# First projections of a two-layer decoder trunk: packing, loading and splitting of the first weights in another order

## The chip, the core and the metric

One core of a Trainium2 chip runs the whole program in one launch. The metric is device time in microseconds (us), the median of three runs. PE is the matrix engine, with its weight load (PEld) shown apart; DVE, ACT and POOL are the vector, scalar and general engines; SP issues most of the loads. Every engine has a queue of its own that it works through in order, and loads can be issued from SP's queue or ACT's.

## The reference, cut to what matters

A decoder trunk of two layers on one sequence of 256 tokens with 1024 channels in float32. Layer 0 has two groups of attention heads behind one input projection; only its beginning matters here.

```python
h = h + even_mixer(rmsnorm(h, even_norm1), even_w_in, ...)      # layer 0
h = h + conv_ffn(rmsnorm(h, ffn_norm[0]), ...)
h = h + odd_mixer(rmsnorm(h, odd_norm1), odd_w_in, ...)         # layer 1
h = h + conv_ffn(rmsnorm(h, ffn_norm[1]), ...)
return rmsnorm(h, final_norm)

def even_mixer(h, w_in, ...):
    qa, ka, va, qd, kd, vd = split_cols(h @ w_in, (512, 512, 512, 512, 512, 512))
    o_a = softmax(qa @ ka.T * 64**-0.5 + relative_bias, causal) @ va     # 8 heads of 64
    o_b = softmax(1) @ vd - lam * softmax(2) @ vd                        # 4 differential heads
    return concat(o_a, o_b) @ w_out
# lam = exp(sum(lp0*lp1)) - exp(sum(lp2*lp3)) + lam_init, from the input diff_lambda
```

## The kernel before, in words

**Numbers.** A float32 product is made of three matmuls. A weight is split into a high part (ACT copies it to a rounded type, `whi`, line 152) and a low part (DVE subtracts, `wlo`, line 153); the activations likewise into `xh` (ACT, line 234) and `xl` (DVE, line 236), both in the tile `xs`. A product is high x xh + high x xl + low x xh, accumulated in one bank (`pd`). All products go through the helper on line 123, so their rows carry that line.

**Norm.** The activations are multiplied by the norm's gain only (`gcol`, a small load on ACT's queue). The factor 1/rms of each token is put on behind the product: squares (`sqt`), their sums over channels by a product with ones (`pss`, PE), scale and epsilon (`rs`, DVE), power -0.5 (`r_col`, POOL), a diagonal matrix (`diag`, DVE), its product with ones (`psb`, PE), and a copy (`r_bc`, DVE). `stats1` (line 555) issues the steps to `diag`, `stats2` (line 559) those behind. `r_q` is `r_bc` times the score scale. `evac_pair` (line 516, operation on 518) multiplies a bank of q or k by it and so makes two heads' `qk`.

**Weights.** All weights lie in memory as chunks of at most 1 MB in the order of a list, PLAN (line 61). A chunk is [128 partitions, k tiles x columns]; a k tile is 128 channels. Three raw buffers (`raw`) rotate, as do four pairs of high and low buffers. `need(name)` (line 170) is called by a step that uses a chunk: it issues raw loads up to three chunks ahead and splits up to two ahead. A raw load waits until the low part of the chunk that had its buffer is done.

**The start.** The first chunks are q0, k0, q1, k1, each 256 columns by all 8 k tiles; then two chunks of v, and so on. x and the chunks q0 and k0 come in four pieces of two k tiles each (`FIRST_KS`, 256 KB a load). Chunk 3 (k1) goes to four small tiles of its own (`raw_t`). Nine warm-up matmuls run on PE, then for each piece xh, xl, the splits of both chunks and 24 matmuls: 96 up to k tile 7. Then come the bias table's row product (`psbt`) and four units: `u1` and `u2` with 24 matmuls each on q1, `u3` and `u4` with 24 each on k1. `stats1` stands at the end of `u2`, `stats2` and three evacuations at the end of `u3`, the fourth at the end of `u4`. Behind them are the units of v and of the later q and k, and `interleave` (line 493) puts the attention of a pair of heads between units: scores (`pS`, PE), bias and maximum (`sc`, `nm`, DVE), exponential (`ex`, ACT), scaling by the sum (`ex`, DVE), transposes (`pT`, PE), their copy (`pt`, ACT), the product with v (`pO`, PE). Task t may not begin before unit `FIRST` = 4.

**Other loads.** `bias_load` (line 327) reads a bias table `Tt` for some heads from memory, on ACT's queue. `loads`, in front of unit 6, issues lam's input (`lam_t`, line 1007) among others, on SP; `lambdas` (line 580), in front of unit 10, works it out on DVE (lines 582, 585, 588, 589) and ACT (line 587).

**What sets the order.** PE's instructions stand as written, in the whole program. For ACT, DVE, POOL and SP the framework's scheduler chooses the order, except in the stretch between the opening of `begin` (a manual schedule, line 977) and `begin.close()` in `u3`, where it is as written. The first loads are written ahead of that opening. Each engine starts an instruction only when those ahead of it in its queue have been started.

## Time and profile before

| | us |
|---|---|
| three runs, median | 603.11 (602.80 to 603.61) |
| profiled execution | 603.49 |
| its span, first to last instruction | 601.7 |
| PE busy | 590.3 |
| DVE busy | 441.5 |
| ACT busy | 348.7 |
| chain that ended last: share of PE | 88% |

The profiled execution is 1.79 us longer than its span. A row of the timeline gives start, duration, engine, source line, operation, output and inputs with their shapes, the count where neighbours are grouped, and in brackets the idle time of the engine ahead of it with what ended that idle time. The chain of waits gives start, duration and what the end waited for. A count of x4 with a time is the time from the first one's start to the last one's end.

### The profile page before, as it was taken

The page shows a single profiled execution, that of the slowest core. Times are in us where ns is not written, and L with a number is a line of the kernel's source. Part 1 is how long each engine was busy: PE and PEld are TensorE (multiplying, and loading weights), DVE is VectorE, ACT ScalarE, POOL GpSimd, SP SyncE. Part 2 cuts the span into 40 slices and gives each one's busy share as a digit, 9 for nine tenths or more (in the row PEclk, how much of TensorE's full clock was granted, in tenths as well). Part 3 has the DMA queues.
Part 4 walks back from the last instruction along what each step waited for, and adds up shares of the span by engine and source line. Part 5 has one row for each costly group of instructions (what it writes and reads, how often), then busy time and mean ns, then how long its engine had stood idle before and what let it go on. Part 6 is the DMA issues. An engine that isn't in the chain of part 4 may idle for free.

```text
span 601.7 us, 10374 instructions
## 1 busy us (share of the span) xinstructions
PE 590.3 (98%) x4076; PEld 544.2 (90%) x4076; DVE 441.5 (73%) x791; ACT 348.7 (58%) x645; POOL 69.6 (12%) x81
## 2 busy tenths in 40 slices
PE   7999999999999999999999999999999999999996
PEld 7988999999999999999999998999988888888885
DVE  5589667689877787777787885658967787777752
ACT  6648557466655565655664674736655566655632
POOL 1000000032101110011033100005111111011110
PEclk9999999999999999999999999999999999999998
DMA  8865653335455545544445434334545544554301
GB/s 300 298 230 217 242 182 148 141 136 191 164 211 210 192 169 199 209 160 167 172 171 205 145 141 141 141 141 162 219 145 209 210 167 183 211 179 171 141 1 71
DMA packets 20265, 106.67 MB, mean 177 GB/s; under 512 B 2478, under 2 KB 5496, under 8 KB 8568
## 3 DMA queue, kind: packets, MB, share of 16 engines
q1 hardware_dynamic: 16424, 101.40, 46.6%
q10 hardware_dynamic: 3632, 4.08, 2.0%
q8 instruction: 32, 0.52, 0.3%
q0 software_dynamic: 160, 0.52, 0.3%
q14 instruction: 17, 0.14, 0.1%
HBM read 104.92 MB, written 1.08 MB: 176 GB/s over the span
## 4 chain that ended last, share of the span: by engine, by line
PE 88%; DVE 4%; issue 3%; POOL 2%; ACT 2%; DMA 1%; SPq 0%; POOLq 0%; ACTq 0%; DVEq 0%
PE pd L123 51%; PE acc L123 26%; PE pv L123 4%; PE pO L123 2%; PE pS L123 2%; DVE wlo L153 2%; DMA raw<-in_wpack_dram 1%; PE puq L123 1%; POOL sqt L245 1%; DVE ex L363 1%; PE pukv L123 0%; DVE sc L353 0%; PE pT L367 0%; PE psb L123 0%; PE pss L123 0%
## 5 line engine op out<-in xcount | busy, mean ns | idle before, releaser
L123 PE MATMUL pd<-xs,whi 128*128 128x256 f32 (+1 forms) x1312 | 330.7, 332 | 2.5 <-ACT whi L152 2.5
L123 PE MATMUL pd<-xs,wlo 128*128 128x256 f32 x928 | 257.1, 282 | 0.0
L153 DVE TENSOR_TENSOR wlo<-raw,whi 128x1024 fp32r<-128x1024 f32 (+1 forms) x193 | 233.8, 1238 | 23.6 <-ACT whi L152 23.5
L123 PEld LDWEIGHTS pd<-xs,whi 128*128 128x128 f32 x1312 | 221.4, 192 | 25.7 <-ACT whi L152 3.1
L152 ACT ACTIVATE whi<-raw 128x1024 fp32r<-128x1024 f32 (+1 forms) x193 | 193.7, 1031 | 60.8 <-PE pd L123 20.9
L123 PEld LDWEIGHTS pd<-xs,wlo 128*128 128x128 f32 x928 | 175.0, 191 | 0.0
L123 PE MATMUL acc<-o,whi 128*128 128x256 f32 x608 | 108.7, 281 | 0.0
L123 PEld LDWEIGHTS acc<-o,whi 128*128 128x128 f32 x608 | 92.7, 188 | 1.0 <-issue 0.2
L123 PE MATMUL acc<-o,wlo 128*128 128x256 f32 x304 | 84.7, 279 | 0.0
L905 ACT ACTIVATE lowp<-pd 128x256 f32<-128x256 f32 x68 | 25.9, 380 | 79.8 <-PE pd L123 79.8
L801 POOL TENSOR_TENSOR ge<-ge,gbuf 128x256 f32<-128x256 f32 x44 | 37.0, 842 | 291.3 <-ACT ge L800 291.3
L906 DVE TENSOR_TENSOR ug<-pd,lowp 128x256 f32<-128x256 f32 x68 | 28.6, 420 | 50.3 <-ACT lowp L905 50.3
L123 PE MATMUL acc<-whi,o 128*128 128x512 f32 (+1 forms) x220 | 58.2, 350 | 0.2 <-ACT o L806 0.2
L123 PEld LDWEIGHTS acc<-o,wlo 128*128 128x128 f32 x304 | 57.1, 188 | 0.0
L123 PEld LDWEIGHTS acc<-whi,o 128*128 128x128 f32 x220 | 38.3, 188 | 7.5 <-ACT o L806 0.7
L123 PE MATMUL acc<-wlo,o 128*128 128x512 f32 (+1 forms) x110 | 38.6, 351 | 0.0
L356 ACT ACTIVATE ex<-sc,nm 128x256 f32<-128x256 f32 (+1 forms) x56 | 24.7, 443 | 17.7 <-DVE nm L353 14.3
L807 DVE TENSOR_TENSOR o<-ge,o 128x256 fp32r<-128x256 f32 x44 | 19.0, 439 | 21.5 <-ACT o L806 21.5
L788 ACT ACTIVATE t<-gbuf,ccol 128x256 f32<-128x256 f32 x44 | 26.4, 601 | 12.1 <-DVE gbuf L929 10.2
L806 ACT ACTIVATE o<-ge 128x256 fp32r<-128x256 f32 x44 | 18.4, 418 | 23.1 <-POOL ge L801 23.0
L123 PE MATMUL pv<-whi,xs 128*128 128x512 f32 x96 | 30.2, 395 | 0.0
L800 ACT ACTIVATE ge<-t 128x256 f32<-128x256 f32 x44 | 17.9, 410 | 15.3 <-DVE t L795 15.3
(153 smaller groups left out, 507.2 us busy)
## 6 DMA issues: line engine op xcount, KB each, us to landing
raw<-in_wpack_dram SPq DMA_DIRECT2D x91, 1024.0 KB, 4.8
raw<-in_wpack_dram SPq DMA_DIRECT2D x6, 256.0 KB, 5.3
raw<-in_wpack_dram SPq DMA_DIRECT2D x3, 512.0 KB, 5.6
Tt<-btab ACTq DMA_DIRECT2D x3, 512.0 KB, 7.1
raw_t<-in_wpack_dram SPq DMA_DIRECT2D x4, 256.0 KB, 6.4
Tt<-btab ACTq DMA_DIRECT2D x1, 1024.0 KB, 10.6
hT<-in_x_dram SPq DMA_DIRECT2D x3, 256.0 KB, 5.3
raw<-in_wpack_dram ACTq DMA_DIRECT2D x2, 256.0 KB, 5.0
```

What stands on the lines that cost most here:

```text
L123: nc.tensor.matmul(o, l, r, start=start, stop=stop, skip_group_check=True)
L152: nc.scalar.activation(hi[:, s], raw, AF.Copy)
L153: nc.vector.tensor_tensor(lo[:, s], raw, hi[:, s].bitcast(F32), op=ALU.subtract)
L245: eng.tensor_tensor(sqs['a'], sqs['a'], t, op=ALU.add)
L356: nc.scalar.activation(e[:, a:b], t[:, a:b], AF.Exp, bias=nm[:, i:i + 1], scale=-1.0, accum_out=den[:, i:i + 1])
L788: nc.scalar.activation(t1, g[:, 2:], AF.Identity, bias=col(f, 3), scale=col(f, 2))
L800: nc.scalar.activation(ge, t3, AF.Gelu)
L801: nc.gpsimd.tensor_tensor(ge, ge, gbuf[f % 3][:, 0, 2:], op=ALU.mult)
L806: nc.scalar.activation(o[:, 0], ge, AF.Copy)
L807: nc.vector.tensor_tensor(o[:, 1], ge, o[:, 0].bitcast(F32), op=ALU.subtract)
L905: nc.scalar.activation(lowp, p[:, S:], AF.Copy)
L906: nc.vector.tensor_tensor(t[:, i], p[:, :S], lowp, op=ALU.add)
```

## The change

It reorders the beginning of layer 0 in five ways; the matmuls, splits and loaded bytes are the same.

1. The first four chunks become q (512 columns) of k tiles 0 to 3 (`eqa`), q of k tiles 4 to 7 (`eqb`), and k likewise (`eka`, `ekb`). `pieces` cuts chunk 0 into four of one k tile, the others into two.
2. `FIRST_KS` is now one k tile each for the first four and two pieces of two: x comes in six loads, and the first 96 matmuls (all q) go in six parts.
3. `begin` opens ahead of the first loads, so that these stand in the written order on SP and ACT.
4. Units `u1` to `u4` become three: `u1` has the 48 matmuls of k tiles 0 to 3 of k, then `stats1`; `u2` 12 matmuls, `stats2`, 12 matmuls, three evacuations; `u3` the last 24 and the fourth evacuation. `FIRST` is 3, and `loads` and `lambdas` stand in front of units 5 and 9.
5. `split_piece(4, ...)` for the first half of chunk 4 stands behind `stats1`; the other half and chunk 5 stand behind the three evacuations.

```diff
-FIRST = 4
+FIRST = 3
-FIRST_KS = ((0, 2), (2, 4), (4, 6), (6, 8))
+FIRST_KS = ((0, 1), (1, 2), (2, 3), (3, 4), (4, 6), (6, 8))
...
-    for n, c in (("q0", 0), ("k0", 512), ("q1", 256), ("k1", 768)):
-        add("e" + n, "we_in", 0, 0, 8, c, 256)
+    for n, c in (("q", 0), ("k", 512)):
+        for i in range(2):
+            add(f"e{n}{'ab'[i]}", "we_in", 0, i * 512, 4, c, 512)
...
-        if i < 2:
-            return n, [slice(a * S, b * S) for a, b in FIRST_KS]
-        step = 512 if i == SMALL_RAW else 1024
+        step = 512 if i in (0, SMALL_RAW) else 1024
...
-    nc.scalar.activation(scr, ones[:, 0:1], AF.Copy)
+    begin = ExitStack()
+    begin.enter_context(tc.manual_schedule(engines={mybir.EngineType.Activation, mybir.EngineType.DVE,
+                                                  mybir.EngineType.Pool, mybir.EngineType.SP}))
...
     load_x(0, nc.sync)
     load_raw(0, 0, nc.scalar)
-    load_raw(1, 0)
-    load_x(1, nc.scalar)
+    nc.scalar.activation(scr, ones[:, 0:1], AF.Copy)
+    load_x(1, nc.sync)
     load_raw(0, 1)
-    load_raw(1, 1, nc.scalar)
-    for part in range(2, len(FIRST_KS)):
-        load_x(part, nc.sync)
-        for i in range(2):
-            load_raw(i, part)
+    load_x(2, nc.scalar)
+    load_raw(0, 2)
+    load_x(3, nc.scalar)
+    load_raw(0, 3)
+    for i in range(2):
+        load_x(4 + i, nc.sync)
+        load_raw(1, i)
     load_raw(2, 0)
...
-    def passmajor(items, ks):
+    def passmajor(name, items, ks):
         for n in range(3):
-            for ap, first, (hi, lo), c in items:
+            for ap, first, c in items:
                 s = slice(c, c + 128)
                 for k in ks:
+                    hi, lo = chunks[name + 'ab'[k // 4]]
                     w, m = ((hi, xh), (hi, xl), (lo, xh))[n]
-                    mm(ap, w[:, k, s], m[:, k], k == 0 and n == 0 and first, k == KD - 1 and n == 2)
+                    mm(ap, w[:, k % 4, s], m[:, k], k == 0 and n == 0 and first, k == KD - 1 and n == 2)
...
         def u1():
-            c = chunks['eq1']
-            p = box['q1'] = bank("pd")
-            colmajor([(p[:, 0:S], True, c, 0)])
+            box['k'] = [bank("pd"), bank("pd")]
+            for ks in ((0, 1), (2, 3)):
+                passmajor("ek", tiles(box['k']), ks)
             split_chunk(3)
...
+            stats1(env)
+            open_split(4)
+            split_piece(4, pieces(4)[1][0])
 
         def u2():
-            p = box['q1']
-            colmajor([(p[:, S:], True, chunks['eq1'], 128)])
-            stats1(env)
-
-        def u3():
-            box['k1'] = bank("pd")
-            colmajor([(box['k1'][:, 0:S], True, chunks['ek1'], 0)])
-            p = box['q1']
+            t = tiles(box['k'])[:2]
+            passmajor("ek", t, (4, 5))
             stats2(env)
             stats_q(env)
+            passmajor("ek", t, (6, 7))
             evac_pair(env, first[0], ('q0', 'q1'), env['r_q'])
-            evac_pair(env, first[1], ('k0', 'k1'), env['r_bc'])
-            evac_pair(env, p, ('q2', 'q3'), env['r_q'])
-            split_chunk(4)
-            split_at[0] = 5
+            evac_pair(env, box['k'][0], ('k0', 'k1'), env['r_bc'])
+            evac_pair(env, first[1], ('q2', 'q3'), env['r_q'])
+            split_piece(4, pieces(4)[1][1])
+            split_chunk(5)
+            split_at[0] = 6
             begin.close()
...
-        before(6, loads)
-        before(10, lambda: lambdas(box['lam']))
+        before(5, loads)
+        before(9, lambda: lambdas(box['lam']))
...
     for part, (a, b) in enumerate(FIRST_KS):
         make_xhat(range(a, b), NORM1[0])
-        for i in range(2):
-            split_piece(i, pieces(i)[1][part])
-        passmajor(items, range(a, b))
+        split_piece(part // 4, pieces(part // 4)[1][part % 4])
+        passmajor("eq", tiles(first), range(a, b))
```

How this moves instructions is seen in each engine's order. On SP at the program's start, `hT` is x and `raw` the chunks; the number behind a name tells buffers apart. Before (`raw_98` is chunk 0, `raw_100` chunk 1, `raw_111` chunk 2):

```order
L200 DMA hT_96<-in_x_dram 128x512
L144 DMA raw_98<-in_wpack_dram 128x512
L200 DMA hT_96<-in_x_dram 128x512
L144 DMA raw_100<-in_wpack_dram 128x512
L144 DMA raw_98<-in_wpack_dram 128x512
L144 DMA raw_100<-in_wpack_dram 128x512
L200 DMA hT_96<-in_x_dram 128x512
L144 DMA raw_98<-in_wpack_dram 128x512
L144 DMA raw_100<-in_wpack_dram 128x512
L144 DMA raw_111<-in_wpack_dram 128x1024
```

And after, with one x load of k tile 0 and one of k tile 1 in the first row, and `raw_99`, `raw_109` and `raw_113` for chunks 0, 1 and 2:

```order
L201 DMA hT_97<-in_x_dram 128x256 x2
L143 DMA raw_99<-in_wpack_dram 128x512 x3
L201 DMA hT_97<-in_x_dram 128x512
L143 DMA raw_109<-in_wpack_dram 128x1024
L201 DMA hT_97<-in_x_dram 128x512
L143 DMA raw_109<-in_wpack_dram 128x1024
L143 DMA raw_113<-in_wpack_dram 128x1024
```

ACT's queue has the first piece of chunk 0 and x of k tiles 2 and 3 now; before, it had the first piece of chunk 0, the second of x and the second of chunk 1. On SP, pieces of two chunks alternated; now one chunk comes whole before the next.

On DVE from the norm's first step to the fourth evacuation, before (`wlo_425` is chunk 4's low part, `wlo_435` chunk 5's):

```order
L252 TENSOR_SCALAR rs_382<-pss_378 128x2
L268 TENSOR_TENSOR diag_385<-ident_85,r_col_381 128x256
L286 COPY r_bc_414<-psb_412 128x256
L564 TENSOR_SCALAR r_q_416<-r_bc_414 128x256
L518 TENSOR_TENSOR qk_418<-pd_156,r_q_416 128x512
L518 TENSOR_TENSOR qk_420<-pd_157,r_bc_414 128x512
L518 TENSOR_TENSOR qk_422<-pd_317,r_q_416 128x512
L153 TENSOR_TENSOR wlo_425<-raw_295,whi_424 128x1024 x2
L153 TENSOR_TENSOR wlo_435<-raw_297,whi_434 128x1024 x2
L518 TENSOR_TENSOR qk_464<-pd_387,r_bc_414 128x512
```

And after (`wlo_385` is chunk 4's, `wlo_427` chunk 5's):

```order
L255 TENSOR_SCALAR rs_379<-pss_375 128x2
L271 TENSOR_TENSOR diag_382<-ident_85,r_col_378 128x256
L152 TENSOR_TENSOR wlo_385<-raw_291,whi_384 128x1024
L289 COPY r_bc_402<-psb_400 128x256
L568 TENSOR_SCALAR r_q_404<-r_bc_402 128x256
L522 TENSOR_TENSOR qk_418<-pd_156,r_q_404 128x512
L522 TENSOR_TENSOR qk_420<-pd_313,r_bc_402 128x512
L522 TENSOR_TENSOR qk_422<-pd_157,r_q_404 128x512
L152 TENSOR_TENSOR wlo_385<-raw_291,whi_384 128x1024
L152 TENSOR_TENSOR wlo_427<-raw_293,whi_426 128x1024 x2
L522 TENSOR_TENSOR qk_460<-pd_314,r_bc_402 128x512
```

One low part of 1024 columns has moved to between `diag` and `r_bc`; three are left between the third and the fourth evacuation.

On SP around lam's load, before (`raw_526` is chunk 7, `raw_867` chunk 11):

```order
L144 DMA raw_526<-in_wpack_dram 128x2048
L144 DMA raw_534<-in_wpack_dram 128x2048
L144 DMA raw_686<-in_wpack_dram 128x2048
L144 DMA raw_785<-in_wpack_dram 128x2048
L1007 DMA lam_t_681<-in_lam_dram 128x256
L144 DMA raw_867<-in_wpack_dram 128x2048
```

And after (`raw_522` is chunk 7, `raw_863` chunk 11):

```order
L143 DMA raw_522<-in_wpack_dram 128x2048
L143 DMA raw_530<-in_wpack_dram 128x2048
L143 DMA raw_682<-in_wpack_dram 128x2048
L143 DMA raw_781<-in_wpack_dram 128x2048
L143 DMA raw_863<-in_wpack_dram 128x2048
L1008 DMA lam_t_677<-in_lam_dram 128x256
L143 DMA raw_984<-in_wpack_dram 128x2048
```

`lam_t`'s load now stands behind chunk 11's raw load, which waits for the last low part of chunk 8 (`wlo_685` after, `wlo_689` before).

## Rows read from the trace of the kernel before

**Rows 1.** The page's first part: busy time of each engine, its share of the span, and its instructions.

```profile
PE 590.3 (98%) x4076; PEld 544.2 (90%) x4076; DVE 441.5 (73%) x791; ACT 348.7 (58%) x645; POOL 69.6 (12%) x81
```

**Rows 2.** Waits of PE over the whole run, and of its weight load from 5 to 70 us: who waited for whom, us in total, times, longest us.

```profile
PE pd L123 <- ACT whi L152: 2.5, 2, 1.7
PE pT L367 <- DVE lam_t L582: 1.1, 1, 1.1
...
PEld pS L123 <- DVE nm L353: 0.4, 1, 0.4
```

**Rows 3.** Timeline of PE through the first 96 matmuls, and the bias product behind them.

```profile
6.98 1.22 PE L123 MATMUL pd<-xs,whi 128*128 128x256 f32 x4 [1.73 <-ACT whi L152]
9.01 2.93 PE L123 MATMUL pd<-xs,whi 128*128 128x256 f32 x12 [0.81 <-ACT whi L152]
11.73 1.91 PE L123 MATMUL pd<-xs,wlo 128*128 128x256 f32 x8
13.44 2.36 PE L123 MATMUL pd<-xs,whi 128*128 128x256 f32 x16
15.63 1.12 PE L123 MATMUL pd<-xs,wlo 128*128 128x256 f32 x8
...
22.44 0.49 PE L123 MATMUL psbt<-oh_t,rb 32*20 32x384 f32 x1
```

**Rows 4.** The stretch of the first 96 matmuls as one window: its length, busy time and count of PE, PEld, DVE, ACT and POOL, then granted clock, the DMA engines' share and GB/s.

```profile
6.98:22.44 15.46, 14.65 (x96) 14.22 (x96) 9.79 (x16) 12.45 (x23) 0.00 (x0) 1.00 1.00 373
```

**Rows 5.** Timeline of ACT at the start.

```profile
5.03 0.91 ACT L234 ACTIVATE xs<-hT,gcol 128x256 fp32r<-128x256 f32 x2 [2.35 <-DMA gcol<-in_small_dram]
6.29 0.63 ACT L152 ACTIVATE whi<-raw 128x512 fp32r<-128x512 f32 x1 [0.36 <-DMA raw<-in_wpack_dram]
8.33 0.63 ACT L152 ACTIVATE whi<-raw 128x512 fp32r<-128x512 f32 x1 [1.40 <-DMA raw<-in_wpack_dram]
```

**Rows 6.** Loads at the start: SP's second issue in its timeline; the same load in the list of issues (queue, count, KB, us from issue to landing); and one piece of the chain of waits (start, us, what).

```profile
1.16 0.42 SPq L144 DMA_DIRECT2D raw<-in_wpack_dram  x1
...
raw<-in_wpack_dram SPq DMA_DIRECT2D x1, 256.0 KB, 4.2
...
2.10 6.20 DMA raw<-in_wpack_dram
```

**Rows 7.** The norm's steps: pieces of the chain of waits (start, us, engine and output), and DVE's timeline at diag and r_bc.

```profile
29.20 0.34 PE pss L123 x4
29.54 2.97 PE pd L123 x24
...
30.58 0.43 DVE L268 TENSOR_TENSOR diag<-ident,r_col 128x256 f32<-128x256 f32 x1 [0.84 <-POOL r_col L253]
...
32.98 0.42 DVE L286 COPY r_bc<-psb 128x256 f32<-128x256 f32 x1 [1.97 <-PE psb L123]
```

**Rows 8.** Timeline of DVE behind the third evacuation: the low parts, the first softmax, and the end of the second pair's.

```profile
35.57 4.62 DVE L153 TENSOR_TENSOR wlo<-raw,whi 128x1024 fp32r<-128x1024 f32 x4
...
40.71 0.42 DVE L353 CUSTOM_DVE_ANT_0 sc<-pS,Tt 128x256 f32<-128x256 f32 x1
...
54.79 1.21 DVE L153 TENSOR_TENSOR wlo<-raw,whi 128x1024 fp32r<-128x1024 f32 x1
55.91 0.55 DVE L363 TENSOR_SCALAR ex<-ex,rd 128x256 f32<-128x256 f32 x2
```

**Rows 9.** Timeline of PE at the transposes of the second pair and at the second product with v.

```profile
54.72 0.27 PE L369 MATMUL pT<-ident,ex 128*128 128x128 f32 x1
54.95 0.30 PE L367 MATMUL pT<-ident,ex 128*128 128x128 f32 x1
...
55.20 0.27 PE L369 MATMUL pT<-ident,ex 128*128 128x128 f32 x1
56.60 0.30 PE L367 MATMUL pT<-ident,ex 128*128 128x128 f32 x1 [1.14 <-DVE lam_t L582]
...
64.48 0.77 PE L123 MATMUL pO<-pt,va 128*64 128x256 f32 x6
```

**Rows 10.** lam and what stands beside it: SP's issue of its load, DVE's and ACT's timelines, and the list of issues for three loads (lam_t's, Tt's, and the raw load issued at 59.8): queue, count, KB, us from issue to landing.

```profile
50.23 0.42 SPq L1007 DMA_DIRECT2D lam_t<-in_lam_dram  x1
...
56.37 0.36 DVE L582 TENSOR_TENSOR lam_t<-lam_t 128x64 f32<-128x64 f32 x2
56.64 0.35 DVE L585 TENSOR_REDUCE lam<-lam_t 128x1 f32<-128x64 f32 x2
...
56.79 0.48 ACT L371 ACTIVATE pt<-pT 128x384 f32<-128x384 f32 x1
57.08 0.37 ACTq L328 DMA_DIRECT2D Tt<-btab  x1
...
57.53 1.06 ACT L152 ACTIVATE whi<-raw 128x1024 fp32r<-128x1024 f32 x1
58.48 0.21 ACT L587 ACTIVATE lam<-lam 128x2 f32<-128x2 f32 x1
...
lam_t<-in_lam_dram SPq DMA_DIRECT2D x1, 128.0 KB, 4.8
...
Tt<-btab ACTq DMA_DIRECT2D x1, 1024.0 KB, 10.6
...
raw<-in_wpack_dram SPq DMA_DIRECT2D x1, 1024.0 KB, 7.6
```

More of the change, by code (lines that the diff above doesn't have):

```diff
@@ L596, in u1 @@
         def u1():
-            c = chunks['eq1']
-            p = box['q1'] = bank("pd")
-            colmajor([(p[:, 0:S], True, c, 0)])
+            box['k'] = [bank("pd"), bank("pd")]
+            for ks in ((0, 1), (2, 3)):
+                passmajor("ek", tiles(box['k']), ks)
             split_chunk(3)
-            split_at[0] = 4
             T.update(bias_load(0, 4, 0))
             T.update(bias_load(4, 4, 4))
+            stats1(env)
+            open_split(4)
+            split_piece(4, pieces(4)[1][0])
         def u2():
-            p = box['q1']
-            colmajor([(p[:, S:], True, chunks['eq1'], 128)])
-            stats1(env)
-        def u3():
-            box['k1'] = bank("pd")
-            colmajor([(box['k1'][:, 0:S], True, chunks['ek1'], 0)])
-            p = box['q1']
+            t = tiles(box['k'])[:2]
+            passmajor("ek", t, (4, 5))
             stats2(env)
             stats_q(env)
+            passmajor("ek", t, (6, 7))
             evac_pair(env, first[0], ('q0', 'q1'), env['r_q'])
-            evac_pair(env, first[1], ('k0', 'k1'), env['r_bc'])
-            evac_pair(env, p, ('q2', 'q3'), env['r_q'])
-            split_chunk(4)
-            split_at[0] = 5
+            evac_pair(env, box['k'][0], ('k0', 'k1'), env['r_bc'])
[3 more added lines that the diff above has]
+            split_at[0] = 6
             begin.close()
@@ L624, in u3 @@
             nc.gpsimd.tensor_tensor(sel, sel, ident, op=ALU.add)
-        def u4():
-            colmajor([(box['k1'][:, S:], True, need('ek1'), 128)])
-            evac_pair(env, box['k1'], ('k2', 'k3'), env['r_bc'])
-        units = [(None, u1), (None, u2), (None, u3), (None, u4)]
+        def u3():
+            need("ekb")
+            passmajor("ek", tiles(box['k'])[2:], range(4, KD))
+            evac_pair(env, box['k'][1], ('k2', 'k3'), env['r_bc'])
+        units = [(None, u1), (None, u2), (None, u3)]
         units += v_units(env, 'eva', 'va')
@@ L976, in trunk @@
         mm(warm[:, :128], ones, ones, True, True)
-    begin = ExitStack()
-    begin.enter_context(tc.manual_schedule(engines={mybir.EngineType.Activation, mybir.EngineType.DVE,
-                                                  mybir.EngineType.Pool, mybir.EngineType.SP}))
     nc.vector.tensor_scalar(subg, gcol[:, SUBLN:SUBLN + 1], 1.0 - LAM_INIT, None, op0=ALU.mult)
@@ L983, in trunk, with tiles @@
     first = [bank("pd"), bank("pd")]
-    items = [(first[c][:, i * S:(i + 1) * S], i == 0, chunks[n], i * 128)
-             for c, n in enumerate(("eq0", "ek0")) for i in range(2)]
+    def tiles(banks):
+        return [(banks[c][:, i * S:(i + 1) * S], i == 0, (2 * c + i) * 128)
+                for c in range(len(banks)) for i in range(2)]
     for part, (a, b) in enumerate(FIRST_KS):
         make_xhat(range(a, b), NORM1[0])
-        for i in range(2):
-            split_piece(i, pieces(i)[1][part])
-        passmajor(items, range(a, b))
+        split_piece(part // 4, pieces(part // 4)[1][part % 4])
+        passmajor("eq", tiles(first), range(a, b))
     pb = bias_rows()
```

## The prediction

> **What bounds the kernel now.** I read the page's busy line first: TensorE (PE) works 98% of the span [rows 1]. An edit that removes no matmul can therefore only gain what PE loses in waits and at a low clock, and the second view, PE's waits over the whole run, says where that is: 2.5 us of "pd" waiting for ACT's high parts at the start and 1.1 us of "pT" behind DVE, with 0.4 us of "pS" on the weight loader [rows 2]. All lie in the first 57 us; behind that PE is full, so what is won or lost by then reaches the end unchanged.
>
> The third view, PE's timeline of the first 96 matmuls, shows the larger loss [rows 3]. The eight that start at 11.73 take until 13.44, 0.2135 us each; the eight that start at 15.63 take until 16.59, 0.120 each. 256 columns in 0.2135 us is the 1.2 GHz level; the granted clock column of that stretch reads 1.00 all the same [rows 4], so I go by the pace. The sixteen from 13.44 to 15.63 fit 2.9 slow ones, which puts the rise at 14.06, 5.05 us after PE resumed at 9.01 with no gap in between. The 96 take 15.46 us [rows 4] against 96 x 0.12 = 11.52: **3.94 us are lost**. Of these 9.01 - 6.98 - 4 x 0.2135 = 1.18 is a gap, some 27.6 slow matmuls x 0.0935 = 2.58, and 0.18 is left over. The gap is a load order: ACT's second high part starts at 8.33 after 1.40 us of waiting for a load [rows 5], the one issued at 2.10 that took 6.20 [rows 6].
>
> The fourth view is DVE from 32.98 on. The norm factor r_bc, three evacuations, four low parts in a row (4.62 us), a fourth evacuation, then softmax from 40.71 [rows 7, 8]. PE reaches its last four transposes at 55.2 and gets the final one at 56.60, after DVE's last ex [rows 8, 9].
>
> **The change, part by part.** No matmul, split or byte goes or comes; all terms are moves in time.
>
> *Start: -0.82.* Now k tile 0 alone starts PE: 128 KB of x and one 256 KB piece of weights. Such a piece, second in line, was issued at 1.16 and landed 4.2 us later, 5.36 [rows 6]. ACT's first xs waits for gcol and starts at 5.03 [rows 5], as it still must; half of its 0.91 us is k tile 0, so the high part runs from about 5.47 to 6.10 (0.63 each [rows 5]), and PE starts 0.06 later as before (6.92 to 6.98): 6.16. Ends: 6.98 if the piece comes no sooner, 5.8 if gcol has play. I take 6.16, since both prices are from rows of the same start.
>
> *No gap, fewer slow matmuls: -1.66.* With queues full this stretch moved 373 GB/s [rows 4], so 384 KB for a k tile come every 1.05 us, while PE eats one in 12 x 0.2135 = 2.56 us. k tile 1 is then there about 6.4 and is wanted at 8.7 less its 0.63 us on ACT; the later ones have more slack. On ACT a k tile costs 0.46 + 0.63 = 1.09 us, also under 2.56. If the clock rises 5.05 us after the gapless start, at 11.21, 23.7 matmuls are slow: 2.21 us, and with a share of the unassigned 0.18, 2.28 in place of 3.94. Each microsecond sooner or later is worth 4.68 x 0.0935 = 0.44; I keep 1 us each way. The bias matmul psbt moves from 22.44 to 19.96, **-2.48**.
>
> Here the loads become smaller, 128 and 256 KB. The Trainium skill (page "DMA: Bandwidth & Descriptors", section "Bandwidth") says to batch loads to 1 MiB or more for 75% of peak, and its fit (section "Anatomy of one DMA") is 2.0 us plus bytes over 436 GB/s; one after the other, an estimate by that page is 4.9 us for a k tile, and the third rival's time would come out. By this trace, with its 256 KB loads in flight together at 373 GB/s [rows 4], the page's figure describes a lone load, and the sum stays at -2.48.
>
> *Norm: +0.2.* Between pss and psb stand 12 matmuls instead of 24. pss' four end at 29.20 + 0.34 = 29.54 and diag is ready at 30.58 + 0.43 = 31.01, 1.47 later; 24 matmuls took 2.97, so 12 take 1.49 [rows 7]. That is a tie, and PE needs 0.14 after a DVE result (56.46 to 56.60 [rows 8, 9]) and a weight load: +0.2, ends 0 and 0.5.
>
> *DVE chain: -1.8.* The words promise low parts of chunks 4 to 6 between the norm's steps; the order shows one of 1.15 us (4.62 / 4 [rows 8]) between diag and r_bc, the others still behind the evacuations, and none of chunk 6 moved. From pss' start r_bc came 32.98 - 29.20 = 3.78 later [rows 7]; now diag is done at 1.81 and the low part at 2.97, with psb's product under 0.5 us behind the 2.03 at which PE comes to it, so r_bc at 3.0: 0.8 sooner, and behind it stands one low part less, 1.15. With -2.48 softmax starts 4.4 sooner while PE comes 2.48 - 0.2 = 2.3 sooner. The pS wait of 0.4 goes [rows 2]. The transposes follow each other every 0.11 us, so the pT waits are 56.60 - 55.20 - 0.11 = 1.29 before the last group and 54.95 - 54.72 - 0.11 = 0.12 before another [rows 9]; in place of them PE arrives near 52.7 and DVE's last ex ends near 56.46 - 4.4 + 0.6 = 52.7, the 0.6 for ACT's exponentials, which now stand behind a table load's wait. Sum -0.4 - 1.4 = -1.8; the end without that gain is 0.
>
> *A new wait: +0.65.* The order puts lam_t's load behind one raw load more. That raw waits for the last low part of its buffer's owner, which ended at 54.79 + 1.21 = 56.00 [rows 8] and now near 51.3, so lam_t is issued near 51.65 rather than at 50.23 [rows 10]. DVE reaches lam_t about 52.4 and stands in order until it lands. Behind it on ACT are lam's exponential, a high part and two pt: 0.62 + 0.21 + 1.06 + 0.48, some 2.4 us [rows 10] to the first pt that PE's second pO needs. That pO was at 64.48 [rows 9] and comes at 64.48 - 2.48 + 0.2 - 1.8 = 60.4 if nothing holds it, so any landing after 58.0 costs PE. Prices for the landing: lam_t itself took 4.8 with the queues nearly free, a raw load issued 2.7 us behind Tt's took 7.6, Tt's own 10.6 [rows 10]. Here Tt goes out some 3.6 us ahead of lam_t, so more of it is through than for the 7.6: I take 7.0, landing at 58.65, a stall of 58.65 + 2.4 - 60.4 = **+0.65**. The ends are 0 (landing 56.4) and 4.2 (62.25).
>
> **Sum:** -0.82 - 1.66 + 0.2 - 1.8 + 0.65 = -3.43. The profiled run took 603.49, 0.38 above the median of 603.11. So 600.06 for such a run, **599.7** against the median.
>
> **The rivals.**
> First, **lam_t is the bound**. For it: Tt's load is under way and a 1 MB raw stands ahead on the same queue. If it lands as late as Tt did, 10.6 after issue, the stall is 4.25 in place of 0.65, the whole gain is gone: 603.3. Against it: a 128 KB load, with Tt started earlier. Chance 0.12.
>
> Second, **the start gives little**: the first piece lands no sooner (6.98) and the clock rises at 14.06 whatever PE does. Then 33 of the 96 are slow, 3.1 us, psbt at 21.67, -0.77. The DVE chain and lam_t come 1.7 later too, the stall stays 0.6, and the sum is -0.77 + 0.2 - 1.8 + 0.6 = -1.7: 601.4. For it: nothing in one trace says from what moment the rise counts. Against: it came after the gap, not after a set number of matmuls. Chance 0.15.
>
> Third, **slower: the pieces come slower than PE eats them.** The places are k tiles 1 to 3, wanted at 8.7, 11.2 and about 13. If each stops PE so that the clock stays at 1.2 GHz through all 96, they take 96 x 0.2135 = 20.5, psbt comes at 26.7, +4.2; with +0.2 - 1.8 and a lam_t stall that stays 0.6, 606.4. It decides once a k tile takes over 2.56 us. For it: the smaller loads. Against: 1.05 us by the row above. Chance 0.05.
>
> Fourth, **the change doesn't do what it says**: with a single low part between the steps, that one delays r_bc instead of filling a hole (psb later, DVE late to it), and the pT and pS waits stay. Then -2.48 + 0.2 is left, lam_t's landing moves later with DVE, and its stall of 0.6 comes on top: -1.7, 601.4. Chance 0.13.
>
> **How the numbers follow.** The forecast has 0.55, from 598.4 (landing in time, a sooner rise) to 601. About 0.2%, 1.2 us, is what a measurement of this kernel can tell from no change. The second and fourth rivals are faster by more than that, at 601.4, and with the upper end of their spread nearly reach 602. The range 598.4 to 602.0 leaves out most of the first rival, the third, and some of both tails, together 0.2. Faster: 0.55 + 0.13 + 0.12 + a part of the first rival where the landing is only half as late, 0.05, gives 0.85. Same: 0.11. Slower: 0.04.
>
> **What would show it.** In the trace of after: first pd near 6.2, the 96 without a gap over 0.1, pace doubling near 11.2, psbt near 20.0; psb waiting for diag 0.1 to 0.3; r_bc 3.0 after pss; no pS or pT wait above 0.5; DVE idle before lam_t's product for 5 to 7 us, ended by a DMA, and PE waiting for pt before the second pO by up to 1.2. Wrong would be: a stall of PE on whi or xs at k tiles 1 to 3, a rise that stays near 14, or new waits behind 65 us, where I count none.

## The result and the profile after

The changed kernel takes **598.94 us** in the median of four runs (598.31 to 599.89) against 603.26 before (602.80 to 603.61): ratio 0.993, 95% interval 0.9912 to 0.9948. In five later runs it took 599.69 (598.60 to 600.02) against 602.86 (17 runs): ratio 0.994, 0.9927 to 0.9953. The profiled execution took 599.55, which is 3.94 less than the profiled one before; its span is 597.8. Of the runs of the kernel before that stand beside e8 to e11 below, one fell in a slow state at 1175.51 us, and the ratios leave it out.

Where those 3.94 lie is read from four points on PE in the two traces: the first `pd`, the bias product `psbt` behind the first 96 matmuls, the second of the two products `pO`, and the end.

| point on PE | before | after | won up to there |
|---|---|---|---|
| first `pd` | 6.98 | 6.52 | 0.46 |
| `psbt` | 22.44 | 19.75 | 2.69 |
| second `pO` | 64.48 | 60.57 | 3.91 |
| end of the execution | 603.49 | 599.55 | 3.94 |

From the second `pO` to the end both take 539.0: behind 65 us nothing changed. The table compares one execution of each kernel; how far the first two rows differ between executions of the same start is seen at e8 and e9.

First the start. PE's timeline of the changed kernel, to be laid beside [rows 3]:

```profile
6.52 2.08 PE L124 MATMUL pd<-xs,whi 128*128 128x256 f32 x8 [1.26 <-ACT whi L151]
8.39 1.05 PE L124 MATMUL pd<-xs,wlo 128*128 128x256 f32 x4
9.24 1.47 PE L124 MATMUL pd<-xs,whi 128*128 128x256 f32 x8
10.55 0.64 PE L124 MATMUL pd<-xs,wlo 128*128 128x256 f32 x4
...
19.75 0.82 PE L124 MATMUL psbt<-oh_t,rb 32*20 32x384 f32 x2
```

Four matmuls from 8.39 to 9.24 take 0.213 each, the 1.2 GHz level; four from 10.55 to 11.02 take 0.12, the 2.4 GHz level. The eight from 9.24 to 10.55 fit 3.7 at the 1.2 GHz level, so the pace doubled near 10.03, 3.5 us after the first `pd`, and no gap stands in the 96: they took 13.23 us where they had taken 15.46 [rows 4].

ACT at the start, beside [rows 5]:

```profile
4.39 0.51 ACT L237 ACTIVATE xs<-hT,gcol 128x256 fp32r<-128x256 f32 x1 [1.24 <-DMA gcol<-in_small_dram]
5.83 0.63 ACT L151 ACTIVATE whi<-raw 128x512 fp32r<-128x512 f32 x1 [0.94 <-DMA raw<-in_wpack_dram]
```

The high part waits for its weights, not for `gcol`. The first piece of weights was issued at 1.17 on ACT's queue. In the kernel before the first piece is also 256 KB on ACT's queue, issued at 1.24. In the list of issues (queue, count, KB, us from issue to landing) it stands before and after as

```profile
raw<-in_wpack_dram ACTq DMA_DIRECT2D x1, 256.0 KB, 5.0
...
raw<-in_wpack_dram ACTq DMA_DIRECT2D x1, 256.0 KB, 4.6
```

The 4.2 of [rows 6] is another load, the second piece on SP's queue.

Then DVE, from the norm's step to the softmax and at lam, beside [rows 7, 8, 10]:

```profile
27.89 0.42 DVE L271 TENSOR_TENSOR diag<-ident,r_col 128x256 f32<-128x256 f32 x1 [0.84 <-POOL r_col L256]
28.23 1.22 DVE L152 TENSOR_TENSOR wlo<-raw,whi 128x1024 fp32r<-128x1024 f32 x1
29.37 0.41 DVE L289 COPY r_bc<-psb 128x256 f32<-128x256 f32 x1
...
31.95 3.48 DVE L152 TENSOR_TENSOR wlo<-raw,whi 128x1024 fp32r<-128x1024 f32 x3
35.35 0.68 DVE L522 TENSOR_TENSOR qk<-pd,r_bc 128x512 f32<-128x512 f32 x1
35.95 0.41 DVE L357 CUSTOM_DVE_ANT_0 sc<-pS,Tt 128x256 f32<-128x256 f32 x1
...
51.75 0.55 DVE L367 TENSOR_SCALAR ex<-ex,rd 128x256 f32<-128x256 f32 x2
58.45 0.36 DVE L586 TENSOR_TENSOR lam_t<-lam_t 128x64 f32<-128x64 f32 x2 [6.15 <-DMA lam_t<-in_lam_dram]
```

One low part stands in the place of the hole of 1.97 us that was ahead of `r_bc` [rows 7]; three follow in a row instead of four. The softmax starts at 35.95 instead of 40.71, 4.76 sooner, and the last `ex` ends at 52.30 instead of 56.46. Then DVE stands 6.15 us for lam's load.

What PE sees of it, beside [rows 9]: the last transposes, the second `pO`, and PE's waits over the whole run.

```profile
52.72 0.27 PE L371 MATMUL pT<-ident,ex 128*128 128x128 f32 x1
...
60.57 1.57 PE L124 MATMUL pO<-pt,va 128*64 128x256 f32 x16
```

```profile
PE pd L124 <- ACT whi L151: 1.3, 1, 1.3
PE warm L124 <- DVE gbuf L779: 1.0, 1, 1.0
PE pss L124 <- POOL sqc L677: 0.6, 1, 0.6
```

The `pT` wait of 1.1 [rows 2] is gone, and PE does not wait at `pO` although DVE stood so long: the copies it needs were ready, as ACT's rows show (the second line is two `pt` in 0.85 us).

```profile
59.21 1.05 ACT L151 ACTIVATE whi<-raw 128x1024 fp32r<-128x1024 f32 x1
60.16 0.85 ACT L375 ACTIVATE pt<-pT 128x384 f32<-128x384 f32 x2
```

### The profile page after: what moved, and what is told of

The parts are those of the page before. It is cut to its first block, busy times and chain, and to the rows that moved or that the text cites. A ratio compares the mean times of both kernels' runs of the same rounds, so it can differ in the third digit from the quotient of the medians.

```text
span 597.8 us, 10369 instructions
## 1 busy us (share of the span) xinstructions
PE 588.8 (98%) x4076; PEld 543.2 (91%) x4076; DVE 441.1 (74%) x789; ACT 348.4 (58%) x643; POOL 69.6 (12%) x81
## 4 chain that ended last, share of the span: by engine, by line
PE 93%; issue 2%; POOL 2%; ACT 1%; DVE 1%; DMA 1%; POOLq 0%; ACTq 0%
PE pd L124 52%; PE acc L124 26%; PE pv L124 6%; PE pS L124 2%; PE pO L124 2%; PE puq L124 1%; DMA raw<-in_wpack_dram 1%; POOL sqt L248 1%; PE pukv L124 1%; PE pT L371 0%; PE pT L372 0%; PE pT L373 0%; PE psb L124 0%; PE pss L124 0%; POOL sqc L677 0%
## 5 line engine op out<-in xcount | busy, mean ns | idle before, releaser
L124 PE MATMUL pd<-xs,whi 128*128 128x256 f32 (+1 forms) x1312 | 326.9, 331 | 1.3 <-ACT whi L151 1.3
L124 PE MATMUL pd<-xs,wlo 128*128 128x256 f32 x928 | 252.7, 282 | 0.0
L124 PEld LDWEIGHTS pd<-xs,whi 128*128 128x128 f32 x1312 | 218.9, 191 | 24.1 <-ACT whi L151 2.2
L124 PEld LDWEIGHTS pd<-xs,wlo 128*128 128x128 f32 x928 | 172.9, 191 | 0.0
```

The source lines that it names most:

```text
L124: nc.tensor.matmul(o, l, r, start=start, stop=stop, skip_group_check=True)
```

## The experiments

Each kernel differs by a few lines from one of the two kernels. Ratios are against runs of the kernel before that were taken together with them: a median of 603.34 (20 runs) for e1 to e4, 602.86 (17 runs) for e5 to e7 and the repeat, 602.94 (17 runs) for e8 to e11. In the diffs, `...` marks what is left out.

**e1: the kernel before with the load order alone.** `begin` opens ahead of the loads, and with that the table load (the `activation` line) moves behind the first weights; the run does not tell the two apart.

```diff
-    nc.scalar.activation(scr, ones[:, 0:1], AF.Copy)
+    begin = ExitStack()
+    begin.enter_context(tc.manual_schedule(...))
...
     load_raw(0, 0, nc.scalar)
+    nc.scalar.activation(scr, ones[:, 0:1], AF.Copy)
     load_raw(1, 0)
...
-    begin = ExitStack()
-    begin.enter_context(tc.manual_schedule(...))
```

> The kernel before with one thing of the change: the first loads stand in the written order on SP and ACT, so that the first piece of chunk 1 goes out ahead of the second piece of chunk 0; pairs of k tiles, packing and units as before. My theory (the 0.81 us gap and the late rise of PE's pace are one loss, and it comes from the load order): PE starts near 6.98 as before, the gap is gone, the pace doubles 3.5 to 5 us after the start, psbt comes near 20.2 to 20.9 in place of 22.44, and all behind it shifts by as much: 601.0 to 601.7. Rival A (the gain of the start comes from the smaller first pieces and the packing): 602.8 or more. Rival B (the pace rises near 14.06 whatever PE does): the gap goes but the matmuls stay slow, psbt near 21.6, 602.4.

Measured: 600.29 (599.93 to 602.71), ratio 0.9963 (0.9949 to 0.9977), 0.7 faster than the lower end of my theory. PE's timeline of e1:

```profile
6.20 2.23 PE L123 MATMUL pd<-xs,whi 128*128 128x256 f32 x16 [0.94 <-ACT whi L152]
...
10.75 1.70 PE L123 MATMUL pd<-xs,whi 128*128 128x256 f32 x12 [0.89 <-ACT whi L152]
...
19.09 0.82 PE L123 MATMUL psbt<-oh_t,rb 32*20 32x384 f32 x2
```

Rival A falls: `psbt` is at 19.09, sooner than the changed kernel's 19.75, so the start's gain needs neither smaller pieces nor the packing. Rival B falls too: the matmuls did not stay slow. But my theory is only half right. The gap did not go, it moved to the next pair of k tiles: the sixteen from 6.20 run at the full pace from the first on, and PE stands 0.89 us in the second pair.

**e2: the changed kernel, lam's load on POOL's queue.**

```diff
-            box['lam'] = late_loads()
+            late_loads()
+        def loads2():
+            box['lam'] = lam_load()
+        before(5, loads2)
...
-        nc.sync.dma_start(lam_t, bass.AP(tensor=lam_p.tensor, offset=lam_p.offset,
+        nc.gpsimd.dma_start(lam_t, bass.AP(tensor=lam_p.tensor, offset=lam_p.offset,
```

> The changed kernel with lam's load on POOL's queue, where no raw load stands ahead of it; the order on DVE and ACT is unchanged. In the changed kernel's trace DVE stands 6.15 us for this load. My theory: that wait ended just in time, PE's second product with v (pO) came 4.56 us behind the first, as in the kernel before, so the time stays that of the changed kernel, 598.9, within 0.5, though DVE's idle 6 us are gone. Rival: the load comes late in some executions and is what makes the 599.6 and 599.9 among the changed kernel's times; then all runs come at 598.3.

Measured: 599.62 (598.90 to 599.94), ratio 0.9944 (0.9932 to 0.9956), 0.2 beyond the 0.5 that my theory allowed and no faster than the changed kernel. DVE comes to lam's product at 51.71 without a wait and PE gains nothing: behind `psbt` this profile takes 579.90, the changed kernel's 579.80. DVE's 6 us of idle time cost nothing there, and the rival (all runs at 598.3) falls. PE's timeline shows something else:

```profile
6.60 1.22 PE L124 MATMUL pd<-xs,whi 128*128 128x256 f32 x8 [1.34 <-ACT whi L151]
...
13.05 2.18 PE L124 MATMUL pd<-xs,whi 128*128 128x256 f32 x16 [0.43 <-ACT whi L151]
```

Here the pace is full from the first `pd`, a k tile lasts 1.44 us, and then k tiles 4 and 5 come too late: PE waits for them.

**e3: the changed kernel with 1 MB more on SP's queue ahead of chunk 11's raw load and lam's load** (a store that nothing reads).

```diff
+        before(6, loads2)
...
+        nc.sync.dma_start(filler, raws[raw_at[0] - 1])
         nc.sync.dma_start(lam_t, bass.AP(tensor=lam_p.tensor, offset=lam_p.offset,
```

> The changed kernel with 1 MB more on SP's queue ahead of chunk 11's raw load and lam's load (a store of a raw buffer to memory that nothing reads). My theory: lam_t lands some 2.5 us later (1 MB at about 400 GB/s), DVE stands that much longer, and as the wait was already used up to the last tenth, PE's second pO moves by the same: about 601.4. Rival (there is slack of a microsecond or more behind lam): under 600.

Measured: 601.84 (600.37 to 603.75), ratio 0.9981 (0.9971 to 0.9991), 2.2 slower than e2. DVE waits 8.12 us, and the wait reaches PE in the middle of the second `pO`:

```profile
60.06 0.88 PE L124 MATMUL pO<-pt,va 128*64 128x256 f32 x8
62.15 1.25 PE L124 MATMUL pO<-pt,va 128*64 128x256 f32 x8 [1.21 <-ACT pt L376]
```

So the wait is real and near its edge, and the rival (a microsecond or more of slack) falls. But it is the second half of this product that needs the late `pt`; the first half, 0.75 us, runs without. That is the slack that the changed kernel lives on.

**e4: the changed kernel with the low part put back behind the evacuations.**

```diff
             open_split(4)
-            split_piece(4, pieces(4)[1][0])
...
+            split_piece(4, pieces(4)[1][0])
             split_piece(4, pieces(4)[1][1])
```

> The changed kernel with the first low part of chunk 4 put back behind the three evacuations (its high part moves with it). My theory: r_bc comes 0.4 to 0.6 sooner, but one low part more (1.15) lies between the evacuations and the softmax, so DVE's last ex ends 0.6 later than in the changed kernel, 0.2 to 0.4 of that reaches PE at the last transposes, and lam's load goes out 0.6 or more later, which PE feels in full: 599.5 to 600.1. Rival (the moved low part makes no difference, the DVE chain gained only by the start): 598.9.

Measured: 601.39 (601.17 to 601.80), ratio 0.9974 (0.9964 to 0.9984), 1.3 over the upper end of my theory. `psbt` is at 19.79, as in the changed kernel, and behind it PE takes 1.6 more, so the rival falls. The transposes wait again, with the same 1.14 us as before (the bracket names the DVE instruction behind the last `ex`; what the transposes read is `ex`):

```profile
52.65 0.30 PE L371 MATMUL pT<-ident,ex 128*128 128x128 f32 x1
...
54.30 0.30 PE L371 MATMUL pT<-ident,ex 128*128 128x128 f32 x1 [1.14 <-DVE lam_t L586]
```

The order far behind differs too, which my theory did not count: the scheduler orders what stands there by itself. It again put chunk 8's last low part ahead of the last `ex`, as in the kernel before, and lam's load again ahead of chunk 11's raw load. So e4 shows what the written line brings together with the order that follows from it, not the 1.15 us of one low part by itself. The run also shows how large the hole is in the changed kernel, with 12 matmuls ahead of `psb`:

```profile
29.14 0.42 DVE L289 COPY r_bc<-psb 128x256 f32<-128x256 f32 x1 [0.79 <-PE psb L124]
```

The hole is 0.79 us here, and a low part takes 1.15: in the changed kernel it overfills the hole and delays `r_bc` by 0.27 (`diag` to `r_bc` takes 1.48 there and 1.21 in e4).

**e5: the changed kernel with pairs of k tiles** (x 256 KB, weights 512 KB a load).

```diff
-FIRST_KS = ((0, 1), (1, 2), (2, 3), (3, 4), (4, 6), (6, 8))
+FIRST_KS = ((0, 2), (2, 4), (4, 6), (6, 8))
...
-        step = 512 if i in (0, SMALL_RAW) else 1024
+        step = 512 if i == SMALL_RAW else 1024
...
```

> The changed kernel with the first four k tiles in two pairs (x 256 KB, weights 512 KB a load) instead of one by one; packing and units stay. My theory (the small first piece is what starts PE early): the first high part now waits for 512 KB and takes 1.04 in place of 0.63, PE starts near 7.6 in place of 6.5, and psbt comes 0.8 to 1.1 later: 600.0 to 600.4. Rival (what counts is the number of loads: a ninth load of the start waits for the first to land, so with fewer and larger ones k tiles 4 to 7 come sooner and PE's wait for them at 12 to 13 us goes): 599.2, as the changed kernel.

Measured: 601.73 (601.11 to 602.45), ratio 0.9979 (0.9970 to 0.9987), 2.0 over the changed kernel and 1.3 over the upper end of my theory.

```profile
7.87 3.62 PE L124 MATMUL pd<-xs,whi 128*128 128x256 f32 x16 [3.00 <-ACT whi L151]
```

PE starts 1.4 later, behind 3.00 us of idle time, and at the low pace (sixteen in 3.46 to the next row, 0.216 each). `psbt` comes at 21.02, 1.2 later than in the changed kernel's repeat. The profiled run, 601.11, is the fastest of the eleven; what the others lost beyond that has no trace. Behind `psbt` it takes 0.3 more than the changed kernel, with lam's load again ahead of chunk 11's raw load. The rival falls: larger loads leave no gap later, but cost more at the front. With 512-column chunks the small first piece is needed; it undoes what the packing costs.

**e6: the changed kernel with 12 warm-up matmuls** (`WARM = 12`).

> The changed kernel with 12 warm-up matmuls instead of 9, so that PE has work until about 6.5 and no idle time over 0.4 us ahead of the first pd. My theory: the pace of the first 96 matmuls differs between executions (risen at 14.06, 10.0, and before the first pd in the profiles so far; once it rose at 4.0, fell again near 7.5 behind 1.9 us of idle time and rose at 10.9), and what sends it down or keeps it down is the idle time ahead of pd. Without that the pace is full from the first pd on or soon behind it in nearly all executions: median 598.3 to 598.8, spread under 1. Rival (the pace rises at a moment that PE's work doesn't set): median and spread as the changed kernel, 599.2, or some tenths more for the longer warm-up.

Measured: 599.31, ratio 0.9936 (0.9920 to 0.9953). Three runs took 598.26 to 598.53, three 600.09 to 600.62: neither theory. The profiled one is of the first three, with 0.61 us idle ahead of `pd`, the 96 at full pace and `psbt` at 18.25. In it lam's wait shows again: the second `pO` takes 1.76 in place of 1.57.

```profile
59.07 1.76 PE L124 MATMUL pO<-pt,va 128*64 128x256 f32 x16
```

PE comes 1.5 us sooner there and lam's load lands only 1.1 sooner, so the slack of the changed kernel is used up. What the three slower runs lost has no trace; their mean granted clock, 0.997 to 0.999, is not apart from that of the three faster, 0.998 to 0.999.

**e7: the changed kernel with 24 matmuls between `pss` and `psb`.** `stats2` moves behind both groups of 12.

> The changed kernel with 24 matmuls between pss and psb, as before, in place of 12. My theory: PE no longer waits for diag (0.25 us), but r_bc comes 0.9 later, DVE's last ex ends 0.9 later, of which PE feels some 0.5 at the last transposes, and lam's load goes out later too: 599.4 to 599.9. Rival (PE's wait for diag is the only effect, the DVE chain has slack): 598.9, 0.2 under the changed kernel.

Measured: 600.78 (598.74 to 601.27), ratio 0.9950 (0.9933 to 0.9967), 1.1 over the changed kernel's repeat and 0.9 over the upper end of my theory; two of the six runs took 598.74 and 599.18, which the one profile (600.78) does not explain. `psbt` is at 19.86 in this profile and in that of the repeat; `r_bc` comes 0.92 later (30.39 against 29.47), the transposes wait

```profile
52.76 0.30 PE L371 MATMUL pT<-ident,ex 128*128 128x128 f32 x1 [0.35 <-DVE rd L362]
53.49 0.30 PE L371 MATMUL pT<-ident,ex 128*128 128x128 f32 x1 [0.21 <-ACT pt L375]
61.36 2.00 PE L124 MATMUL pO<-pt,va 128*64 128x256 f32 x16
```

and the second `pO` takes 2.00 instead of 1.57, since lam's load is later too. In this profile the rival falls: the 12 matmuls are worth the 0.25 us for which PE waits on `diag`.

**The changed kernel again**, for its spread.

> The changed kernel once more, for its spread in the same call. My theory: from the second pO to the end it takes 539.0 as in every profile so far, and what differs between executions is the pace of the first 96 matmuls: median 599.0 to 599.4, from 598.3 to 600. Rival (a second wait behind the start, lam's, comes and goes): the distance from the second pO to the end stays, but first to second pO is over 4.6 in this profile.

Measured: 599.69 (598.60 to 600.02). `pO` to `pO` is 4.56, the second `pO` to the end 599.66 - 60.68 = 538.98: the distances are as my theory had them, and lam's wait does not show in this profile; the median was 0.3 over my bounds. That the pace is what differs between executions this run does not show: the eight matmuls from 9.18 to 10.65 fit 5.4 at the 1.2 GHz level, so it rose at 10.3 here, close to the 10.0 of the first profile.

**e8: the kernel before with the low part alone** (its second half and chunk 5 written behind the evacuations, as in the change).

```diff
             stats1(env)
+            open_split(4)
+            split_piece(4, pieces(4)[1][0])
...
-            split_chunk(4)
-            split_at[0] = 5
+            split_piece(4, pieces(4)[1][1])
+            split_chunk(5)
+            split_at[0] = 6
```

> The kernel before with only the low part moved: the first half of chunk 4 is split behind stats1, its second half and chunk 5 behind the three evacuations; start, packing and units stay. My theory: the low part fits whole into DVE's 1.97 us hole ahead of r_bc, DVE is 1.15 us earlier behind it, and the two waits of the transposes (1.4 us together) shrink to 0.3 or less, with lam's load still ahead of chunk 11's: 601.6 to 602.0 against some 603.1. Rival (the transposes' wait in the changed kernel went because of the start, not of the low part): 603.1.

Measured: 602.16 (600.95 to 602.69), ratio 0.9984 (0.9975 to 0.9993). The transposes' wait falls from 1.14 to 0.21:

```profile
54.25 0.30 PE L367 MATMUL pT<-ident,ex 128*128 128x128 f32 x1 [0.21 <-DVE lam_t L582]
```

The rival falls: the low part does it, not the start. The median moved 0.8, near the 0.9 that this wait lost, and stays 0.2 over my bounds. PE's timeline shows one thing more, since the first loads are those of the kernel before, unchanged:

```profile
6.64 0.73 PE L123 MATMUL pd<-xs,whi 128*128 128x256 f32 x4 [1.58 <-ACT whi L152]
8.52 2.93 PE L123 MATMUL pd<-xs,whi 128*128 128x256 f32 x12 [1.15 <-ACT whi L152]
...
21.07 0.82 PE L123 MATMUL psbt<-oh_t,rb 32*20 32x384 f32 x2
```

With the same start `psbt` came at 22.44 in the profile of the kernel before. So two executions of one start differ by 1.4 us, which is half of the 2.69 that the table of the result shows at `psbt`.

**e9: e1 and e8 together**, without the packing.

> The kernel before with both parts that need no new packing: the written load order at the start (which gave 600.3 alone) and the moved low part. My theory: the two gains lie in different stretches and add up, so 600.3 less 1.1 to 1.4: 598.9 to 599.2, as fast as the changed kernel or faster, without its packing and its smaller pieces. Rival (with an earlier start DVE is late anyway): 600.3.

Measured: 599.23 (598.79 to 599.31), ratio 0.9934 (0.9921 to 0.9946). The gains add up, and the interval holds both ratios of the changed kernel: its packing, small pieces and three units bring nothing that can be told from e9. The profiles agree, taken apart at `psbt`:

| profile | `psbt` | from `psbt` to the end |
|---|---|---|
| before | 22.44 | 581.05 |
| e8, low part alone | 21.07 | 580.06 |
| e1, load order alone | 19.09 | 581.04 |
| e9, both | 19.21 | 580.06 |
| changed | 19.75 | 579.80 |
| changed, repeat | 19.86 | 579.80 |

The last column depends on what stands behind the start and hardly on the execution: the low part brings 0.99 there, the change as a whole 1.25. At `psbt` the changed kernel is not ahead of e1 and e9.

**e10: the kernel before with 14 warm-up matmuls** (`WARM = 14`).

> The kernel before with 14 warm-up matmuls instead of 9, so that PE works until 7.0 or so and the 1.7 us of idle time ahead of the first pd is gone; the 0.8 us gap behind the first four stays. My theory: the 2.58 us that the first 96 lose by pace in the profiled run fall to 1 or less, and the start is 0 to 0.3 later: 601.3 to 602.0. Rival (the gap behind the first four keeps the pace down, or the rise is not set by PE's work): 603.0.

Measured: 601.12 (600.85 to 602.76), ratio 0.9971 (0.9960 to 0.9982). Nothing but warm-up was added, and 1.8 us are gone, 0.2 more than my theory had; by the median the rival falls. The profiled run is the slowest of the seven, so the gain of the other six has no trace. What this one shows is the case of the rival: PE stands still behind the first four, and the pace is down. PE's timeline and two windows of it (columns as in [rows 4]):

```profile
6.53 0.74 PE L123 MATMUL pd<-xs,whi 128*128 128x256 f32 x4
9.02 2.84 PE L123 MATMUL pd<-xs,whi 128*128 128x256 f32 x12 [1.75 <-ACT whi L152]
```

```profile
9.02:12.90 3.88, 3.88 (x19) 3.88 (x20) 3.86 (x8) 3.72 (x9) 0.00 (x0) 0.56 1.06 393
13.03:21.70 8.67, 8.67 (x74) 8.59 (x72) 5.07 (x8) 7.91 (x14) 0.00 (x0) 1.00 1.02 382
```

The four at 6.53 run at full pace. Behind the 1.75 us of idle time the granted clock averages 0.56 up to 12.90, with nineteen matmuls in 3.88 us, then it is 1.00.

**e11: the changed kernel with 14 warm-up matmuls and lam's load on POOL's queue.**

> The changed kernel with 14 warm-up matmuls and lam's load on POOL's queue: what the runs so far point to. My theory: with no idle time left ahead of the first pd in any execution and no wait behind lam the times of the faster half of the 12-matmul kernel, 598.3, are the median, spread under 1: 597.9 to 598.6. Rival (the other half, 600.1 to 600.6, has another cause than idle time): two groups again, median 599.3 or more.

Measured: **598.39** (598.12 to 599.11), ratio 0.9922 (0.9908 to 0.9935), the lowest median of all. PE's timeline:

```profile
1.04 6.05 PE L124 MATMUL warm<-ones 128*128 128x128 f32 x28 [1.04 <-DVE gbuf L783]
6.85 1.20 PE L124 MATMUL pd<-xs,whi 128*128 128x256 f32 x8
...
18.57 0.82 PE L124 MATMUL psbt<-oh_t,rb 32*20 32x384 f32 x2
```

The 96 take 11.72 us, 0.2 over 96 x 0.12. The rival falls. Against the changed kernel, 599.66 in the median of its nine runs, it is 1.3 us; the runs were taken at different times, the intervals of the ratios overlap, and two things were changed at once.

## Why the prediction held, step by step

The forecast was 599.7 in a range of 598.4 to 602.0; the medians were 598.94 and 599.69. Most mechanisms were those that it names, in their places. Four terms were mis-sized and in part they cancel, so that 599.7 met the second median to 0.01 is luck.

- **Start, -0.82: -0.46 in these two traces, and nothing that can be told from chance.** The step that failed is the price of the first piece, 4.2 us from [rows 6]: that row is the second piece, on SP's queue. The piece that PE waits for goes out on ACT's queue with 256 KB before and after, and the traces do not show it sooner. It landed 5.0, 4.7 and 4.6 us after issue in the three traces with the first loads of the kernel before (before, e8, e10), and 4.6 to 5.0 in the eight with those of the changed kernel. The first `pd` was at 6.98, 6.64 and 6.53, and at 6.45 to 6.89.
- **Fewer slow matmuls, -1.66: -2.23.** The gap went as forecast, 1.18. The pace rose 3.5 us after the first `pd`, not 5.05: 15.7 matmuls of 96 were slow, not 23.7 and not the 27.6 of before, which is 1.1 us. Other profiles of this start have them all fast (e2, e3), or fast, slow and fast again (e4), and with the start of the kernel before e8 has some 13 slow. One trace gave no price for this: the stretch varies between executions, which the ends of 1 us each way were too narrow for. The Trainium skill (page "TensorE: Matmul & The Clock Gate", section "Part 1: The HAM clock gate") says that the same kernel shows different numbers of slow matmuls from run to run; the profiles here agree, with 15.7 and none for one and the same start.
- **No gap, 1.05 us for a k tile.** Right at the low pace only. At the full pace PE eats a k tile in 1.44 us, and e2 shows a wait of 0.43 for k tile 4. SP's timeline of the changed kernel fits that: chunk 1's first half is issued only at 5.83, when the first piece of chunk 0 has landed (1.17 + 4.6), so the loads were not all in flight as the term assumed. That the one waits for the other is read from the two times.

```profile
3.85 0.33 SPq L201 DMA_DIRECT2D hT<-in_x_dram  x1
5.83 0.33 SPq L143 DMA_DIRECT2D raw<-in_wpack_dram  x1
```

- **Norm, +0.2: +0.25.** `pss` to the first `pS` takes 6.95 in the changed kernel, 6.70 before. The weight load of `psb` waits 0.2 for `diag`. `r_bc` comes 3.02 after `pss`, as forecast; before it was 3.94 by PE's timeline, where `pss` starts at 29.04, and not the 3.78 that the prediction counts from the chain's 29.20.
- **DVE chain, -1.8: -1.4.** The transposes' 1.4 are gone, and e8 shows that the moved low part does it; in e4, without it, they wait again. The 0.4 ahead of the second `pS` stayed: PEld's row there has the same idle time with no releaser.

```profile
40.47 0.30 PEld L124 LDWEIGHTS pS<-qk 64*128 64x128 f32 x4 [0.35 <-issue]
```

  The step that failed took the releaser `nm` [rows 2] for the cause of that 0.4. An idle time that stays when its releaser comes more than 2 us sooner had another cause; which, the runs don't show.
- **New wait, +0.65: 0.** The landing was right: forecast 58.65, DVE started at 58.45, and DVE's 6.15 us of idle time were forecast as 5 to 7. The step that failed is who waits: the late `pt` feed only the second half of the second `pO`, so a landing after 58.0 does not cost at once; there are 0.75 us more. That the term came out at 0 is a near thing: e6, with an earlier start, pays 0.2, and e3 shows the cost further behind the edge. The first rival had the right mechanism; its landing 10.6 us after issue did not come, lam's load took 7.2.
- **The second rival** (the start gives little) was right in its first half, that the first piece lands no sooner. Its second half, a rise at 14.06 whatever PE does, falls by the profile (10.0) and by e1 (all fast from 6.20). **The third** falls: no k tile kept PE at the low pace, and e5, with the larger loads, was 2.0 slower. The Trainium skill (page "DMA: Bandwidth & Descriptors", section "Anatomy of one DMA — SWDGE (gpsimd) path") gives the fit that the prediction sets beside this rival for loads issued through GpSimd. The loads here go out on SP and ACT, and no row shows the fit for one that is alone: lam's 128 KB took 4.8 us with the queues nearly free [rows 10]. **The fourth** was right that one low part moves and that it delays `r_bc`, by 0.27 (e4), and wrong in what follows: one low part less stands behind, and it alone brings 0.8 (e8), where it fits whole into the hole.

**What stays open.** What sets the moment at which the pace doubles. With more warm-up the times fell (e10, e11), and in e6's and e11's profiles all 96 are fast; but so they are in e1, e2, e3 and e9 with nine warm-up matmuls. In e10 and e8 the pace fell behind 1.75 and 1.15 us of idle time; behind 1.34 and 1.64 it was up (e2, e3), and behind 1.26 it was down (the changed kernel). So that idle time takes the pace down is argued and not shown. And why three of e6's runs took 600.1 or more: it could be lam's wait, which already shows in the faster profile and which e11 took away together with the idle time, or the pace. Not tried: e11 with lam's load left on SP.

## What to carry to other kernels

At the start of a kernel, look at the pace of matmuls (start to start) and not at busy time: here 2.6 of the 3.9 us lost in the first 96 were matmuls at the low clock, in a stretch where PE was 100% busy, and five more warm-up matmuls took 1.8 us off the kernel before (e10). Profile one start more than once before a term of it is priced: at `psbt` two executions differed by 1.4. A price for a wait is taken from the load that is waited for, on its own queue. A hole in a chain of small steps can be filled with work that is due later anyway; it pays by what then comes sooner behind the chain. Where a scheduler chooses the order of loads, read the order: written out, it brought as much without the new packing (e9) as with it.

## What was not expected of the hardware

The granted clock column reads 1.00 in stretches that run at the low pace from the beginning. The changed kernel from 6.52 to 10.08 reads 1.00, with 17 matmuls in 3.56 us; e4, whose pace was up, went down and came up again, reads 0.50 where it was down, with 18 in 3.30 us:

```profile
6.52:10.08 3.56, 3.56 (x17) 3.56 (x17) 2.92 (x6) 2.61 (x6) 0.00 (x0) 1.00 1.01 365
```

```profile
7.50:10.80 3.30, 3.30 (x18) 3.30 (x17) 2.63 (x6) 2.33 (x6) 0.00 (x0) 0.50 1.00 352
```

So a 1.00 ahead of the first change of clock in a trace is no measurement; 0.21 us for 256 columns is.
